# A rotary embedding kernel: one queue for all loads with a new opening, and five tiles added on TensorE instead of four

## The chip, the cores and the metric

The kernel runs on one core of a Trainium2 chip. Times are device microseconds (us) of one execution. A run is called fast or slow by its time against the fastest of the same kernel; only fast runs are compared. The kernel before takes 164.6 us; one of its first three runs took 231.49 us and is not used.

A core has five engines with instruction streams of their own: TensorE (PE in the profile), VectorE (DVE), ScalarE (ACT), GpSimd (POOL) and SyncE (SP). Here SyncE and ScalarE also issue the transfers between HBM and on-chip memory; 16 DMA engines carry them out.

## The reference

```
x: (8, 2048, 8, 64) float32      cos, sin: (2048, 32) float32
x1, x2 = x[..., :32], x[..., 32:]
out1 = x1 * cos - x2 * sin
out2 = x1 * sin + x2 * cos
return concatenate([out1, out2], axis=-1)
```

The tables depend on the position alone and are shared by batch and heads. 33.55 MB are read as x, 0.52 MB as tables, and 33.55 MB written.

## The kernel before

x is cut into 16 slabs of 2 MB (128 partitions x 4096 elements), each rotated in place in one of nine buffers and stored from there. A slab is two tiles of 2048 columns. A tile of kind "A" is done by GpSimd (x times sin, the two halves exchanged, into `t2`) and DVE (x times cos into `t1`, then `t1 + t2`). For kind "B" TensorE adds instead, by two products with the identity summed in PSUM, and ScalarE copies the sum back in four copies. For kind "C" DVE makes both products and TensorE adds them, so GpSimd does nothing.

```
    NBUF = 9                         # slab buffers
    ...
    def cuts(i):                     # how slab i is loaded; HD = 512 columns, UNIT = 2048
        if i == 0:
            return [HD, HD, 2 * HD, UNIT]
        return [SLAB]

    def pieces(i):                   # how slab i is computed (and the last one stored)
        if i == 0:
            return [HD, HD, 2 * HD, UNIT]
        if i == last:
            return [UNIT, 2 * HD, HD, HD]
        return [UNIT, UNIT]
    ...
    nc.scalar.dma_start(out=cos_sb, in_=cos_src)
    for i in range(NBUF):
        load(i)                      # on nc.sync; sin comes right after the first piece of slab 0
    ...
    kinds = {}
    for i in (5, 10):
        kinds |= {(i, 0): "C", (i, UNIT): "B"}
    ...
            # in rotate(), kind "B"; "C" is alike
            for j in range(n // C):
                ...
                nc.tensor.matmul(o, eye, t1[:, cs], start=True, stop=False)
                nc.tensor.matmul(o, eye, t2[:, cs], start=False, stop=True)
                keep(nc.scalar.copy(xt[:, cs], o))
    ...
    LAG = 2

    def store(i, lo, n):             # on ScalarE's DMA queue
        keep(nc.scalar.dma_start(out=ov[...], in_=xts[i][:, lo : lo + n]))

    for i in range(last + 1):
        if i == last:
            for k in range(i - LAG, i):
                store(k, 0, SLAB)
        for lo, n in spans(pieces(i)):
            rotate(i, lo, n)
            if i == last:
                store(i, lo, n)
        if LAG <= i < last:
            store(i - LAG, 0, SLAB)
        if i > LAG and i - LAG - 1 + NBUF <= last:
            load(i - LAG - 1 + NBUF)
```

ScalarE takes its instructions in order, so the store of slab 3, which the program writes after `rotate(5)`, stands behind the eight copies of slab 5. And load 9 needs the buffer of slab 0, so it waits until store 0 has landed, and so on.

Of the kernel before, what the change touches and what calls it, by code (L numbers as in the profile page):

```python
# [10 lines left out]
def kernel(  # L11
# [7 lines left out]
    nc = tc.nc  # L19
# [4 lines left out]
    B, S, H, D = x.shape  # L24
    Dh = D // 2
    P = 128
    HD = H * D
# [4 lines left out]
    SLAB = SL * HD  # L32
    UNIT = 4 * HD
# [5 lines left out]
    cos_src = cos.rearrange("(q r) d -> q r d", q=P)  # L39
# [10 lines left out]
    cos_sb = const_pool.tile([P, R, Dh], f32, tag="cb")  # L50
# [9 lines left out]
    xts = {}  # L60

    def cuts(i):
        if i == 0:
            return [HD, HD, 2 * HD, UNIT]
        return [SLAB]

    def pieces(i):
        if i == 0:
            return [HD, HD, 2 * HD, UNIT]
        if i == last:  # L70
            return [UNIT, 2 * HD, HD, HD]
        return [UNIT, UNIT]

    def spans(sizes):
        lo = 0
        for n in sizes:
            yield lo, n
            lo += n

    def load(i):  # L80
        b, l = slabs[i]
        xt = xpool.tile([P, SLAB], f32, tag="xt", name=f"xt{i}")
        for lo, n in spans(cuts(i)):
            nc.sync.dma_start(
                out=xt[:, lo : lo + n],
                in_=xv[b, :, l * SLAB + lo : l * SLAB + lo + n],
            )
            if i == 0 and lo == 0:
                nc.sync.dma_start(out=sin_sb, in_=sin_src)
        xts[i] = xt  # L90

    nc.scalar.dma_start(out=cos_sb, in_=cos_src)
    for i in range(NBUF):
        load(i)

# [2 lines left out]
        out=eye,  # L98
        in_=eye,
# [12 lines left out]
        return dataclasses.replace(a, ap=[a.ap[0][:], a.ap[1][:], [0, n], a.ap[-1][:]])  # L112

    kinds = {}
    for i in (5, 10):
        kinds |= {(i, 0): "C", (i, UNIT): "B"}

    def rotate(i, lo, n):
        b, l = slabs[i]
# [69 lines left out]
# [12 lines that stand above are left out]
# [30 lines left out]
```

## Time and profile before

| | before |
|---|---|
| time, median | 164.63 us |
| span of the profiled execution | 163.0 us |
| moved by DMA | 67.66 MB |
| DVE busy / GpSimd busy / ScalarE busy / TensorE busy | 143.4 / 139.4 / 12.0 / 33.3 us |

First the busy tenths of DVE and of the 16 DMA engines, and the rate, in 40 equal slices of the span (4.08 us each):

```profile
DVE  0587999999999999999899999999999999999900
...
DMA  4999999999999999999999999999999999999995
GB/s 137 383 432 442 406 398 426 438 438 418 438 434 426 430 434 430 426 434 438 422 428 438 424 422 446 430 414 446 434 422 430 442 422 422 446 426 430 434 402 207
```

The DMA engines are at 90% or more in every slice but the first and the last. The same as windows; columns are the stretch, its length, the busy time of the engines, the granted TensorE clock, the DMA share and the rate:

```profile
core 0: us, PE busy (x) PEld busy (x) DVE busy (x) ACT busy (x) POOL busy (x), PEclk, DMA share, GB/s
20.00:24.00 4.00, 0.00 (x0) 0.00 (x0) 3.86 (x3) 0.00 (x0) 4.00 (x3) 1.00 0.97 377
66.00:72.00 6.00, 6.00 (x15) 2.66 (x14) 5.83 (x4) 2.35 (x4) 5.05 (x3) 1.00 1.01 434
126.00:132.00 6.00, 0.00 (x0) 0.00 (x0) 5.88 (x3) 0.00 (x0) 6.00 (x3) 0.50 1.01 431
136.00:156.00 20.00, 0.00 (x0) 0.00 (x0) 18.10 (x12) 0.00 (x0) 12.93 (x10) 0.50 1.00 430
```

The stretch from 136 to 156 us has only stores, that from 66 to 72 only loads: 430 to 434 GB/s either way. That is the limit. The Trainium skill, page "DMA: Bandwidth & Descriptors", Specifications, gives 435 GB/s as the fabric's ceiling, and this trace agrees. (Slices and short windows can read more, because a packet counts whole where it starts.) 67.66 MB at 430 GB/s are 157.3 us. Below, "lost" time is worked out from the trace's DMA packets so: the length of a stretch, less the bytes moved in it divided by 429.5 GB/s, an estimate of the sustained rate, close to the 430 from 136 to 156 us. Before loses 3.2 us while starting, 0.44 us in a slow patch from 19.75 to 21.75, 0.7 us at the end, and nothing else.

Next ScalarE's timeline: start, length, and what it was. A line with ACTq is a group of DMA issues, its length the time from the first issue to the end of the last.

```profile
17.85 19.24 ACTq L183 DMA_DIRECT2D out_dram<-xt  x3
62.24 0.59 ACT L176 COPY xt<-o 128x512 f32<-128x512 f32 x1 [55.27 <-DVE t L144]
...
74.83 0.59 ACT L158 COPY xt<-o 128x512 f32<-128x512 f32 x1 [1.13 <-PE o L157]
74.83 6.93 ACTq L183 DMA_DIRECT2D out_dram<-xt  x5
106.85 0.59 ACT L176 COPY xt<-o 128x512 f32<-128x512 f32 x1 [31.44 <-PE o L173]
...
119.32 0.59 ACT L158 COPY xt<-o 128x512 f32<-128x512 f32 x1 [1.13 <-PE o L157]
119.38 35.97 ACTq L183 DMA_DIRECT2D out_dram<-xt  x11
```

Three stores are issued by 37 us. The next leave at 74.83, with the last copy of slab 5: 38 us without a store. The same happens before 119.38. Nothing is lost, because loads are still queued: the trace's landings have load 11, the last that could be queued without store 3, land at 79.74, and the last load of all at 123.86. The margins are 4.9 and 4.5 us. The loads do wait for stores; here is the largest entry of SyncE's own waits (total us, times, longest):

```profile
SPq L84 <- DMA out_dram<-xt: 86.4, 7, 31.9
```

### The profile page before, as it was taken

How to read it: one execution, taken by the hardware profiler on the slowest of the kernel's cores; microseconds unless marked ns; L12 is line 12 of the kernel's file. 1: busy time of each engine (PE TensorE's matmuls, PEld its weight loads, DVE VectorE, ACT ScalarE, POOL GpSimd, SP SyncE). 2: the span in 40 equal slices, each digit the busy share in tenths (PEclk: the TensorE clock that was granted, in tenths of full speed). 3: DMA queues.
4: the chain of work that ended last, by engine and by line, in shares of the span. 5: the costliest groups of instructions: out<-in, count | busy, mean ns of one | idle time of the engine just before them, and what ended most of it. 6: DMA issues, size and time to landing. Idle time of an engine off the chain costs nothing. (4 is left out here: it accounts for less than half of the span.)

```text
span 163.0 us, 480 instructions
## 1 busy us (share of the span) xinstructions
PE 33.3 (20%) x64; PEld 13.4 (8%) x64; DVE 143.4 (88%) x71; ACT 12.0 (7%) x20; POOL 139.4 (86%) x74
## 2 busy tenths in 40 slices
PE   0000000000000079993000000899920000000000
PEld 0000000000000024440000000244400000000000
DVE  0587999999999999999899999999999999999900
ACT  3300000000000002232000000022410000000000
POOL 1599999999999999799999999956999999995000
PEclk9999999999999999999555555579997555555555
DMA  4999999999999999999999999999999999999995
GB/s 137 383 432 442 406 398 426 438 438 418 438 434 426 430 434 430 426 434 438 422 428 438 424 422 446 430 414 446 434 422 430 442 422 422 446 426 430 434 402 207
DMA packets 5763, 67.66 MB, mean 415 GB/s; under 512 B 640, under 2 KB 640, under 8 KB 1664
## 3 DMA queue, kind: packets, MB, share of 16 engines
q1 hardware_dynamic: 2880, 33.82, 49.5%
q10 hardware_dynamic: 2880, 33.82, 48.7%
q14 instruction: 3, 0.02, 0.0%
HBM read 34.08 MB, written 33.55 MB: 415 GB/s over the span
## 5 line engine op out<-in xcount | busy, mean ns | idle before, releaser
L138 POOL TENSOR_TENSOR t<-xt,sin_sb 128x1024 f32<-128x1024 f32 (+2 forms) x34 | 70.7, 2081 | 10.8 <-DVE xt L151 6.3
L144 DVE TENSOR_TENSOR t<-xt,cos_ps 128x2048 f32<-128x2048 f32 (+2 forms) x36 | 73.9, 2056 | 1.0
L138 POOL TENSOR_TENSOR t<-xt,nsin 128x1024 f32<-128x1024 f32 (+2 forms) x34 | 70.8, 2082 | 0.0
L151 DVE TENSOR_TENSOR xt<-t,t 128x2048 f32<-128x2048 f32 (+2 forms) x32 | 64.8, 2025 | 5.6 <-POOL t L138 2.1
L172 PE MATMUL o<-t,eye 128*128 128x512 f32 x16 | 11.3, 800 | 85.8 <-DVE t L144 85.8
L176 ACT COPY xt<-o 128x512 f32<-128x512 f32 x8 | 4.7, 586 | 94.5 <-DVE t L144 55.3
L172 PEld LDWEIGHTS o<-t,eye 128*128 128x128 f32 x16 | 3.9, 256 | 90.6 <-issue 90.6
L156 PE MATMUL o<-t,eye 128*128 128x512 f32 x16 | 8.2, 592 | 0.0
L157 PE MATMUL o<-t,eye 128*128 128x512 f32 x16 | 8.2, 592 | 0.0
L173 PE MATMUL o<-t,neye 128*128 128x512 f32 x8 | 6.2, 862 | 0.2 <-DVE t L161 0.2
L158 ACT COPY xt<-o 128x512 f32<-128x512 f32 x8 | 4.7, 586 | 9.0 <-PE o L157 9.0
L108 DVE COPY cos_ps<-cos_sb 128x512 f32<-128x512 f32 x1 | 0.7, 694 | 5.0 <-DMA cos_sb<-in_cos_dram 5.0
L161 DVE TENSOR_TENSOR t<-xt,sin_ps 128x2048 f32<-128x2048 f32 x2 | 4.6, 2281 | 0.0
L173 PE MATMUL o<-t,eye 128*128 128x512 f32 x8 | 4.1, 592 | 0.0
L157 PEld LDWEIGHTS o<-t,eye 128*128 128x128 f32 x16 | 3.0, 190 | 3.8 <-issue 3.8
L156 PEld LDWEIGHTS o<-t,eye 128*128 128x128 f32 x16 | 3.0, 190 | 3.8 <-issue 3.8
L173 PEld LDWEIGHTS o<-t,neye 128*128 128x128 f32 x8 | 2.0, 278 | 4.9 <-issue 3.3
L173 PEld LDWEIGHTS o<-t,eye 128*128 128x128 f32 x8 | 1.5, 190 | 1.9 <-issue 1.9
L106 ACT ACT_TABLE_LOAD x1 | 1.3, 1283 | 1.2 <-PEq L215 1.2
L106 ACT ACTIVATE nsin<-sin_sb 128x512 f32<-128x512 f32 x1 | 0.6, 630 | 3.2 <-DMA sin_sb<-in_sin_dram 3.2
L109 ACT COPY sin_ps<-sin_sb 128x512 f32<-128x512 f32 x1 | 0.6, 579 | 0.0
L96 POOL MEMSET eye<- 128x128 f32 x1 | 0.2, 205 | 0.3 <-POOLq L215 0.3
(6 smaller groups left out, 1.0 us busy)
## 6 DMA issues: line engine op xcount, KB each, us to landing
xt<-in_x_dram SPq DMA_DIRECT2D x15, 2048.0 KB, 27.6
out_dram<-xt ACTq DMA_DIRECT2D x15, 2048.0 KB, 15.3
xt<-in_x_dram SPq DMA_DIRECT2D x1, 1024.0 KB, 7.8
out_dram<-xt ACTq DMA_DIRECT2D x1, 1024.0 KB, 10.3
xt<-in_x_dram SPq DMA_DIRECT2D x2, 256.0 KB, 4.3
xt<-in_x_dram SPq DMA_DIRECT2D x1, 512.0 KB, 5.8
out_dram<-xt ACTq DMA_DIRECT2D x1, 512.0 KB, 8.9
out_dram<-xt ACTq DMA_DIRECT2D x2, 256.0 KB, 7.6
```

Source lines behind the costliest of these rows:

```text
L106: nc.scalar.mul(nsin, sin_sb, -1.0)
L108: nc.vector.tensor_copy(cos_ps, cos_sb)
L138: nc.gpsimd.tensor_mul(out=t2u[:, :, u, :].rearrange("p (r h) d -> p r h d", h=H), in0=xu[:, :, 1 - u, :].rearrange("p (r h) d -> p r h d" ...
L144: nc.vector.tensor_mul(out=t1.rearrange("p (r k d) -> p r k d", r=nr, d=Dh), in0=xk, in1=rep(cos_ps[:, r0 : r0 + nr, :], 2 * H),)
L151: keep(nc.vector.tensor_add(out=xt, in0=t1, in1=t2))
L156: nc.tensor.matmul(o, eye, t1[:, cs], start=True, stop=False)
L157: nc.tensor.matmul(o, eye, t2[:, cs], start=False, stop=True)
L158: keep(nc.scalar.copy(xt[:, cs], o))
L161: nc.vector.tensor_mul(out=t2.rearrange("p (r k d) -> p r k d", r=nr, d=Dh), in0=xk, in1=rep(sin_ps[:, r0 : r0 + nr, :], 2 * H),)
L172: nc.tensor.matmul(o, eye, t1u[:, gs, u, :], start=True, stop=False)
L173: nc.tensor.matmul(o, eye if u else neye, t2u[:, gs, 1 - u, :], start=False, stop=True)
L176: keep(nc.scalar.copy(xu[:, gs, u, :], o.rearrange("p (g d) -> p g d", d=Dh)))
```

## The change

The intent, as far as the diff tells it: larger first loads in one queue, no DMA issue on ScalarE at the start, and a fifth tile taken off DVE.

```diff
     def cuts(i):
-        if i == 0:
-            return [HD, HD, 2 * HD, UNIT]
-        return [SLAB]
+        return [UNIT, UNIT] if i == 0 else [SLAB]
     def pieces(i):
         if i == 0:
-            return [HD, HD, 2 * HD, UNIT]
+            return [2 * HD, 2 * HD, UNIT]
         if i == last:
-            return [UNIT, 2 * HD, HD, HD]
+            return [UNIT, 2 * HD, 2 * HD]
 ...
             if i == 0 and lo == 0:
+                nc.sync.dma_start(out=cos_sb, in_=cos_src)
                 nc.sync.dma_start(out=sin_sb, in_=sin_src)
 ...
-    nc.scalar.dma_start(out=cos_sb, in_=cos_src)
 ...
-    for i in (5, 10):
+    for i in (4, 11):
         kinds |= {(i, 0): "C", (i, UNIT): "B"}
+    kinds[(8, 0)] = "B"
```

## The prediction

> **What bounds the kernel now.** The 16 DMA engines. The page's slices show DMA at 90% or more in all but the first and last of 40, and windows from 8 us on move 420 to 450 GB/s whether loads, stores or both run. 67.66 MB at about 429 GB/s is 157.5 us of the 163.0 us span. The Trainium skill ("DMA: Bandwidth & Descriptors", Specifications) gives 435 GB/s as fabric ceiling; the trace agrees. Compute is nearly as long (DVE 143.4 us, GpSimd 139.4 us) but ends at 155.0, with some 6 us of stores still queued. So DVE time saved is worth nothing by itself; the queues must never run dry.
>
> **Why they could.** A load from slab 9 on needs an earlier store to land, and ScalarE issues stores in order, behind its PSUM copies. Timeline: stores of slabs 0 to 2 issue at 17.9, 27.3, 36.8, then none until 74.8, behind the eight copies of slab 5 (62.2 to 75.4, 1.72 us apart, paced by TensorE). The queued loads last until 79.7. It repeats with slab 10: stores 8 and later wait until 119.4; the last load lands at 123.9. Margins of 4 to 5 us.
>
> **What the change does.**
> 1. Start: x comes as 1 MB, with cos and sin behind it. The skill (same page, "Issuing engines are not separate DMA queues") says other issuing engines save only issue time: here 0.41 us. But sin, which GpSimd needs, has 1.57 MB ahead of and in it, not 0.79: I expect its landing near 7.2 us (5.6 before), and the first slab done about 1.5 us later. Larger packets fill the ramp 0.3 us better.
> 2. One more tile added on TensorE: 2.3 us off DVE, four copies (about 8 us with TensorE's slow start) on ScalarE.
> 3. The blocked stretches move. ScalarE's built order: stores 0, 1, copies of slab 4, stores 2 to 5, copies of slab 8, stores 6 to 8, copies of slab 11, stores 9 on.
>
> **Costing it.** I carried the measured pitches (4.73 us per 2048-column tile on DVE, 4.57 on GpSimd, 1.72 per copy) and 429 GB/s through both orders; for before this gives store 8 at 118.6 (measured 119.4).
> - First dry point: only loads 0 to 10 and stores 0, 1 can be queued, 13 slabs, gone near 68. Store 2 issues near 67. Margin about zero: 0 to 1 us idle.
> - Slab 8: stores 6 to 8 issue near 93. No loss.
> - Second: all 16 loads and stores 0 to 8, gone near 127. Slab 11 is one slab later than slab 10 was; the copies end near 127.5, so store 9 starts moving near 129. About 2 us idle. This decides: from there seven stores, 14.7 MB, 34.2 us, and about 1 us to land.
> Last landing near 164.2 instead of 162.2.
>
> **Prediction:** 166.5 us (+1.1%); 8 in 10 between 164.4 and 168.2. Faster by over 2%: 0.01; within 2%: 0.86; slower by over 2%: 0.13.
>
> **What would show it.** Right: the slices show DMA dipping near 127 to 129 us and perhaps near 68; no store issues between about 94 and 127; DVE ends near 153; sin lands about 1.5 us later. Wrong: DMA at 9 throughout and about 164.3 us.
>
> **What would make it wrong.** The margins are estimates of about 1 us. If the first slab is done as early as before, or the copies run faster, the gaps close and the time stays at 164.3. If copies of slab 11 start later (GpSimd setting the pace and eating the DVE saving), the gap grows by as much, to 168 or more.

## The result, and the profile after

The changed kernel takes 167.5 us (167.31 to 167.66, four runs). The ratio to before is 1.0175 (95% interval 1.0155 to 1.0195). Ratios here are the mean time of one kernel's fast runs over the mean of the other's fast runs of the same rounds, so they are not quite the ratio of the medians quoted. The prediction was 166.5 us with a range of 164.4 to 168.2, and within 2%: it held, and the time was 1 us above its centre.

The same lines of the page, after (slices of 4.15 us):

```profile
DVE  0449999999999999999999999999999999999000
...
DMA  5999999999999999999999999999998999999995
GB/s 186 417 457 423 419 312 443 435 439 431 407 439 443 435 435 411 387 439 399 403 443 419 419 415 435 435 431 431 415 435 344 379 439 395 431 443 439 397 408 212
```

DMA dips to 8 in slice 31, where the rate is 344 GB/s and then 379; slice 6 has 312. ScalarE's timeline:

```profile
19.29 9.79 ACTq L182 DMA_DIRECT2D out_dram<-xt  x2
54.16 0.58 ACT L175 COPY xt<-o 128x512 f32<-128x512 f32 x1 [45.97 <-PE o L172]
...
67.15 0.58 ACT L157 COPY xt<-o 128x512 f32<-128x512 f32 x1 [1.13 <-PE o L156]
67.16 4.91 ACTq L182 DMA_DIRECT2D out_dram<-xt  x4
88.55 0.59 ACT L157 COPY xt<-o 128x512 f32<-128x512 f32 x1 [20.81 <-DMA out_dram<-xt]
...
94.55 0.58 ACT L157 COPY xt<-o 128x512 f32<-128x512 f32 x1 [1.13 <-PE o L156]
94.56 3.29 ACTq L182 DMA_DIRECT2D out_dram<-xt  x3
115.08 0.58 ACT L175 COPY xt<-o 128x512 f32<-128x512 f32 x1 [19.94 <-PE o L172]
118.03 0.58 ACT L175 COPY xt<-o 128x512 f32<-128x512 f32 x1 [2.37 <-PE o L172]
...
128.33 0.58 ACT L157 COPY xt<-o 128x512 f32<-128x512 f32 x1 [1.13 <-PE o L156]
128.39 25.29 ACTq L182 DMA_DIRECT2D out_dram<-xt  x9
```

The stretches without a store are now from 29.08 to 67.16 and from 97.85 to 128.39 (the ends of the issues before them are from the trace). The same four windows as before:

```profile
20.00:24.00 4.00, 0.00 (x0) 0.00 (x0) 3.88 (x2) 0.00 (x0) 4.00 (x3) 1.00 1.03 324
66.00:72.00 6.00, 1.12 (x3) 0.19 (x1) 5.86 (x3) 0.61 (x2) 6.00 (x3) 0.80 1.00 390
126.00:132.00 6.00, 2.29 (x6) 0.75 (x4) 5.66 (x4) 1.17 (x2) 6.00 (x4) 0.92 0.79 330
136.00:156.00 20.00, 0.00 (x0) 0.00 (x0) 16.68 (x10) 0.00 (x0) 11.71 (x8) 0.50 1.02 432
```

Between 126 and 132 us the rate is 330 instead of 431. In windows of 1 us it reads 279 from 127, 0 from 128, and 508 from 129. By the packets, no data packet starts from 127.97 to 129.23, and none is in flight from 128.6 to 129.2.

The balance, as lost time in us (worked out from the packets as above):

| stretch | before | after | difference |
|---|---|---|---|
| opening, to 8 us | 3.23 | 2.46 | -0.77 |
| slow patch after the first store (20 to 25) | 0.44 | 1.11 | +0.67 |
| at store 2 (68.25 to 69.75) | 0 | 0.49 | +0.49 |
| at 78.25 to 79.5 | 0 | 0.27 | +0.27 |
| hole at store 9 (127.5 to 129.5) | 0 | 1.36 | +1.36 |
| last packets, and all small losses | 0.7 | 1.2 | +0.5 |
| last packet ends at | 161.85 | 164.40 | +2.55 |

The last but one row is what the others leave. The difference of the medians is 2.9 us. The rows say where time was lost, not what each cure would give back: bytes that did not move before 127 us are still queued then, so an early loss should make the hole behind slab 11 shorter (argued, not tested alone).

The opening did move the start of compute, as GpSimd's first product shows, before and then after:

```profile
5.74 0.72 POOL L138 TENSOR_TENSOR t<-xt,sin_sb 128x256 f32<-128x256 f32 x1 [4.44 <-DMA sin_sb<-in_sin_dram]
```

```profile
7.00 2.47 POOL L137 TENSOR_TENSOR t<-xt,sin_sb 128x512 f32<-128x512 f32 x2 [5.70 <-DMA sin_sb<-in_sin_dram]
```

It waits for sin in both, 1.26 us longer after. The first slab is done, and its store issued, at 19.29 instead of 17.85.

### The profile page after: what moved, and what is told of

Read it like the earlier page. It is cut to its first block, busy times and chain, and to the rows that moved or that the text cites. A ratio compares the mean times of both kernels' runs of the same rounds, so it can differ in the third digit from the quotient of the medians.

```text
span 165.8 us, 498 instructions
## 1 busy us (share of the span) xinstructions
PE 44.2 (27%) x80; PEld 17.8 (11%) x80; DVE 140.3 (85%) x66; ACT 14.3 (9%) x24; POOL 138.9 (84%) x70
## 5 line engine op out<-in xcount | busy, mean ns | idle before, releaser
L137 POOL TENSOR_TENSOR t<-xt,sin_sb 128x1024 f32<-128x1024 f32 (+1 forms) x32 | 70.5, 2205 | 8.2 <-DMA sin_sb<-in_sin_dram 5.7
L143 DVE TENSOR_TENSOR t<-xt,cos_ps 128x2048 f32<-128x2048 f32 (+1 forms) x34 | 73.4, 2167 | 0.9
L137 POOL TENSOR_TENSOR t<-xt,nsin 128x1024 f32<-128x1024 f32 (+1 forms) x32 | 70.7, 2209 | 0.0
L150 DVE TENSOR_TENSOR xt<-t,t 128x2048 f32<-128x2048 f32 (+1 forms) x29 | 62.2, 2144 | 5.9 <-POOL t L137 2.5
L171 PE MATMUL o<-t,eye 128*128 128x512 f32 x16 | 12.0, 843 | 66.3 <-DVE t L143 66.3
L155 PE MATMUL o<-t,eye 128*128 128x512 f32 x24 | 14.2, 676 | 17.6 <-DVE t L143 17.6
L156 PE MATMUL o<-t,eye 128*128 128x512 f32 x24 | 13.2, 633 | 0.0
L171 PEld LDWEIGHTS o<-t,eye 128*128 128x128 f32 x16 | 3.9, 257 | 71.3 <-issue 71.3
L175 ACT COPY xt<-o 128x512 f32<-128x512 f32 x8 | 4.7, 585 | 74.9 <-PE o L172 74.9
L157 ACT COPY xt<-o 128x512 f32<-128x512 f32 x12 | 7.0, 585 | 34.1 <-DMA out_dram<-xt 20.8
L155 PEld LDWEIGHTS o<-t,eye 128*128 128x128 f32 x24 | 5.0, 212 | 24.3 <-issue 24.3
L172 PE MATMUL o<-t,neye 128*128 128x512 f32 x8 | 6.8, 943 | 0.1
L156 PEld LDWEIGHTS o<-t,eye 128*128 128x128 f32 x24 | 5.0, 210 | 6.9 <-issue 6.9
L172 PE MATMUL o<-t,eye 128*128 128x512 f32 x8 | 4.1, 592 | 0.0
L172 PEld LDWEIGHTS o<-t,eye 128*128 128x128 f32 x8 | 1.5, 190 | 1.9 <-issue 1.9
```

What stands on the lines that cost most here:

```text
L137: nc.gpsimd.tensor_mul(out=t2u[:, :, u, :].rearrange("p (r h) d -> p r h d", h=H), in0=xu[:, :, 1 - u, :].rearrange("p (r h) d -> p r h d" ...
L143: nc.vector.tensor_mul(out=t1.rearrange("p (r k d) -> p r k d", r=nr, d=Dh), in0=xk, in1=rep(cos_ps[:, r0 : r0 + nr, :], 2 * H),)
L150: keep(nc.vector.tensor_add(out=xt, in0=t1, in1=t2))
L171: nc.tensor.matmul(o, eye, t1u[:, gs, u, :], start=True, stop=False)
L172: nc.tensor.matmul(o, eye if u else neye, t2u[:, gs, 1 - u, :], start=False, stop=True)
L175: keep(nc.scalar.copy(xu[:, gs, u, :], o.rearrange("p (g d) -> p g d", d=Dh)))
```

## The experiments

The theory: DMA is the limit; the changed order makes ScalarE issue stores so late that the queues run dry, above all behind the copies of slab 11. Rival A: the later opening (1.4 us) makes everything later. Rival B: the fifth tile itself costs the time, by its TensorE and ScalarE work or by a lower clock.

All twelve runs gave results equal to the reference's.

### Stores ahead of the copies (e1)

The same work on every engine. Only ScalarE's order changes: a slab that has a TensorE tile (4, 8, 11) is preceded by every store that is ready.

```diff
+    nxt = 0
     for i in range(last + 1):
-        if i == last:
-            for k in range(i - LAG, i):
-                store(k, 0, SLAB)
+        if i == last or kinds.get((i, 0)):
+            while nxt < i:
+                store(nxt, 0, SLAB)
+                nxt += 1
 ...
-        if LAG <= i < last:
-            store(i - LAG, 0, SLAB)
+        if LAG <= i < last and nxt <= i - LAG:
+            store(nxt, 0, SLAB)
+            nxt += 1
```

> The changed kernel, but each slab with a TensorE tile (4, 8, 11) is preceded in ScalarE's order by every store that is ready, instead of followed by it; TensorE, DVE and GpSimd do the same work. Theory (queues run dry behind the copies): no hole in DMA near 68 and near 128, store 9 issues near 106 instead of 128, time 163.6 to 164.3 us, below the kernel before because the opening ramp stays 0.8 us better. Rival A (the later opening makes all later): still 167. Rival B (the added TensorE tile, its copies or the lower clock cost the time): still 167.

Measured: 164.61 us (164.47 to 164.74), ratio to before 0.9998 (0.9983 to 1.0013). The page's DMA lines and the stores on ScalarE's timeline:

```profile
DMA  5999999999999999999999999999999999999994
GB/s 183 419 445 435 435 318 423 439 427 443 423 435 431 423 439 431 419 443 427 427 439 427 437 425 427 435 427 439 427 423 439 431 427 435 427 443 423 429 408 200
```

```profile
19.31 28.69 ACTq L182 DMA_DIRECT2D out_dram<-xt  x4
...
67.05 15.76 ACTq L182 DMA_DIRECT2D out_dram<-xt  x4
...
94.44 14.48 ACTq L182 DMA_DIRECT2D out_dram<-xt  x3
115.11 0.59 ACT L175 COPY xt<-o 128x512 f32<-128x512 f32 x1 [20.70 <-PE o L172]
...
127.61 0.59 ACT L157 COPY xt<-o 128x512 f32<-128x512 f32 x1 [1.13 <-PE o L156]
128.23 25.48 ACTq L182 DMA_DIRECT2D out_dram<-xt  x7
```

The copies of slab 11 run at the same time as in the changed kernel (115.11 to 128.20, against 115.08 to 128.91), but stores 8 to 10 were issued between 94.44 and 108.92, so DMA has work: no slice but the ends is below 9. TensorE is busy 42.0 us (44.2 in the changed kernel), ScalarE 14.3 in both, and the first slab is as late (store 0 at 19.31). So neither the fifth tile nor the late opening costs the time; both rivals fall as the main cause.

Nor does the clock cost it by itself. In the changed kernel TensorE began slab 11 slowly: the granted clock was 0.50 from 115 to 117 us, and the first two copies are 2.95 us apart, where 1.72 is the steady spacing. e5 (below: e1 with cos on ScalarE's queue) begins slab 11 as slowly, with the same clock and copies 2.97 us apart, and still moves 431 GB/s between 126 and 132 us. But with the stores behind the copies the slow start counts: by these spacings it put off store 9 by 1.2 us (an estimate), and 1.36 us were lost in that execution.

The time lies above the range expected (163.6 to 164.3), because the gain over before did not come: the opening is 0.8 us better, but the slow patch at 21.5 to 24.5 takes 0.97 us where before lost 0.44. In the profiled run the last packet ends 0.5 us earlier than before's (161.35); of that the medians keep 0.1.

### Only slab 11's stores ahead (e9)

```diff
-        if i == last or kinds.get((i, 0)):
+        if i in (11, last):
```

(against e1; slabs 4 and 8 keep the changed order)

> The changed kernel with only stores 9 and 10 moved ahead of the copies of slab 11; slabs 4 and 8 keep the changed order. Theory: the hole at 127.5 to 129.5 (1.4 us) goes, the slow patches near 68 and 78 (0.75 us) stay: 165.5 to 166.3 us. If the hole near 128 was only a symptom of what happened at 68: no gain, 167.

Measured: 165.59 us (165.46 to 166.16), ratio 1.0064 (1.0038 to 1.0091). Two windows:

```profile
66.00:72.00 6.00, 0.66 (x2) 0.00 (x0) 5.86 (x3) 0.59 (x1) 6.00 (x3) 0.73 0.99 423
126.00:132.00 6.00, 1.84 (x5) 0.53 (x3) 5.66 (x4) 1.17 (x2) 5.83 (x4) 0.85 0.99 423
```

Stores 9 and 10 left at 99.49 and 108.52, the hole at 128 is gone (423 against 330 GB/s), and the median is 1.9 us lower. So the hole is not a mere symptom of what happened near 68, where the edit changes nothing. Not all of the 1.9 us need be the hole's, though. In this execution store 2 left at 66.71, not at 67.16, and the loss near 68 stayed away too (423 against 390 GB/s), which was not expected. The last packet ends 1.87 us earlier than in the changed kernel's trace; the hole had cost 1.36 us there and the loss near 68 0.49. The margin near 68 is that thin. What differs is how slowly TensorE begins after idling: the first two copies of slab 4 are 2.69 us apart in the changed kernel's trace, 2.27 in that of e9, 1.95 in that of e1, and 1.72 is the steady spacing.

### Without the tile in slab 8 (e4)

```diff
-    kinds[(8, 0)] = "B"
```

> The changed kernel without the fifth tile (first half of slab 8), so less TensorE and ScalarE work and 2.3 us more on DVE. Theory: slab 11 is reached about 2.7 us later, store 9 issues near 131, the hole grows to about 4 us: 169.5 to 170.5 us. Rival B (the added tile costs the time): faster than 167.5, toward 165. Rival A: 167.5.

Measured: 168.6 us (167.85 to 169.48), ratio 1.0242 (1.0196 to 1.0288). By the page and the timeline:

```profile
DMA  5999999999999999999999999999993699999996
GB/s 184 422 453 426 422 324 430 426 426 434 434 430 434 434 434 426 430 430 391 422 422 432 436 418 434 434 430 418 418 438 145 281 406 438 438 438 434 406 410 250
```

```profile
130.75 25.25 ACTq L181 DMA_DIRECT2D out_dram<-xt  x9
```

Less work on TensorE and ScalarE (and more on DVE) made it slower still, as the theory said and rival B denied: DVE's 2.3 us return before slab 11, stores 9 to 12 leave from 130.75, and 4.26 us are lost between 127.0 and 131.75 (1.36 in the changed kernel). The size was overstated: the median lies 0.9 us below the range expected. The trace shown is of the slowest of four runs. So the fifth tile, taken by itself, helps: it brings slab 11 forward. What hurts is where the pairs stand: e2, next, has the same opening and four tiles in slabs 5 and 10 and takes 165 us.

### The old tiles with the new opening (e2), the new tiles with the old opening (e3)

e2 is the changed kernel with `for i in (5, 10)` and no tile in slab 8; e3 is the kernel before with `for i in (4, 11)` and the tile in slab 8.

> The changed opening and pieces, with the old four TensorE tiles (slabs 5 and 10). Theory: store 8 issues near 120.5 with the loads lasting to about 121, so a hole of 0 to 1.5 us in all: 164.0 to 165.4 us. Rival A (the opening costs it): 167 or more. Rival B (the tiles cost it): 163.8.

> The old opening and pieces, with the five TensorE tiles of the change. Theory: compute is 1.4 us earlier, so store 9 issues near 126.5 and the hole there shrinks from 1.4 to about 0.5 us: 165.0 to 166.0 us. Rival A (the opening costs it): 164.6. Rival B (tiles): 167.

e2: the profiled execution (169.64 us) is not read. The four fast runs are 164.75 to 165.68, ratio 1.0027 (0.9998 to 1.0057). So the opening does not explain the 2.9 us: rival A falls here too. e3: 165.71 us (164.88 to 166.13), ratio 1.0058 (1.0026 to 1.009), inside the range expected. But its profiled execution is its fastest (164.88) and shows no hole. In it TensorE began slab 11 without a slow start (the granted clock was 1.00 from 115 to 117 us): the first two copies are 1.72 us apart, and store 9 left at 125.78. In the changed kernel's trace they are 2.95 apart.

```profile
113.70 0.59 ACT L178 COPY xt<-o 128x512 f32<-128x512 f32 x1 [19.27 <-PE o L175]
115.42 0.58 ACT L178 COPY xt<-o 128x512 f32<-128x512 f32 x1 [1.13 <-PE o L175]
...
125.78 3.20 ACTq L185 DMA_DIRECT2D out_dram<-xt  x4
```

Store 9 left 2.6 us earlier than in the changed kernel, 1.4 by the opening and 1.2 by the quick start. That the slower runs of e3 have the hole is argued, not shown.

### The order of stores where there was no hole (e11)

The edit of e1, made to the kernel before.

> The kernel before with its stores moved ahead of the copies in the same way as e1. It had no hole in DMA, so the theory gives nothing to win: 164.5 to 164.8 us, no hole, loss of 0.4 us near 20 as before. If issuing stores early is worth something by itself: below 164.2.

Measured: 164.86 us (164.62 to 164.97), ratio 1.0011 (0.9996 to 1.0027). Early stores were worth nothing by themselves here; they paid where the queues would run dry. Its slow patch cost 0.67, more than the 0.4 expected.

### The slow patch after the first store (e5 to e8, e10, e12)

The balance showed a loss that nobody had predicted: some 2 us after the first store is issued, the loads in flight slow down for 2 to 3 us, before the first store's packets show (in the changed kernel the store is issued at 19.29 and its first packet starts at 23.80; until then single packets of 16 KB take up to 1.36 us instead of 0.61). Six runs tried to move it. All but e6 start from e1.

e8 exchanges stores 0 and 1, so the first store leaves at 29.0 us:

```diff
+        if i == LAG + 1:
+            store(1, 0, SLAB)
+            store(0, 0, SLAB)
+            nxt = 2
-        if LAG <= i < last and nxt <= i - LAG:
+        elif LAG + 1 < i < last and nxt <= i - LAG:
```

> e1 with stores 0 and 1 exchanged, so that the first store is issued at 28.8 us instead of 19.3. If the slow patch belongs to the first store, it moves to about 31 to 34 us; if it belongs to the loads in flight at that time, it stays at 21.5 to 24.5. No verdict on time is asked.

e5 undoes one part of the change, e6 does so without e1's order, and e7 issues a tiny store early:

```diff
 e5 and e6
-                nc.sync.dma_start(out=cos_sb, in_=cos_src)
+    nc.scalar.dma_start(out=cos_sb, in_=cos_src)      # before the loads
 e7
+    warm = const_pool.tile([P, 4], f32, tag="warm")
+    nc.vector.memset(warm, 0.0)
+    nc.scalar.dma_start(out=ov[0, :, 0:4], in_=warm)  # overwritten by store 0
```

> e1 with one part of the change undone: cos is again loaded by ScalarE's queue. Question: in every kernel with the new opening the loads run slowly for 3 us (about 1.0 us of transfer lost, 21.5 to 24.5) about 2 us after the first store is issued; with the old opening it is 2 us (about 0.5 lost). Theory Q (the first use of ScalarE's DMA queue costs it, and cos used to be that use): the loss falls to about 0.5 and the time to 164.0. Rival (it comes with the order and size of the first loads): still 1.0 lost, 164.6.

> The changed kernel with cos back on ScalarE's queue and nothing else. Whatever it does to the early slow patch, the hole near 128 is set by when store 9 is issued, so what is won early is lost there: 167.2 to 167.6, the hole larger by the gain. If the early loss counted in the changed kernel by itself: 166.9 or less.

> e1 with a 2 KB store (128 partitions of 16 bytes, overwritten later by slab 0) issued on ScalarE's queue within the first us, before there is load traffic. Theory Q: the slow patch at 21.5 falls from 1.0 us lost to 0.5 or less (below 0.2 if the first write matters too): 163.7 to 164.2. Rival: 1.0 lost still, 164.6.

e10 stores slab 0 in its three pieces as they are ready; e12 issues the same three pieces in reverse order, the 1 MB one first, when slab 0 is done:

```diff
 e10
-            if i == last:
+            if i in (0, last):
                 store(i, lo, n)
 e12
+        if i == 0:
+            for lo, n in reversed(list(spans(pieces(0)))):
+                store(0, lo, n)
```

> e1 with slab 0 stored in three pieces (512 KB, 512 KB, 1 MB), the first issued near 12 us. The slow patch belongs to the first store: it should start near 14 us. If it is a cost of the first time the queue is filled, whatever the size, it is again about 1.0 us and the time 164.6; if it grows with the first store's size, it is 0.5 or less and the time 164.0 to 164.3.

> e10 with the three stores of slab 0 in reverse order, so that the first of them (1 MB) is issued at 19.3 us as in e1, not at 12. If smaller first stores cure the slow patch (its length goes with the first store's size): loss near 0.5 us or less, time 164.1 to 164.3. If the earlier time cured it: loss 0.9 to 1.0 us again, time 164.6.

Windows of e1, then e8, then e10, then e12:

```profile
20.00:24.00 4.00, 0.00 (x0) 0.00 (x0) 3.90 (x2) 0.00 (x0) 4.00 (x3) 1.00 1.02 332
```

```profile
20.00:24.00 4.00, 0.00 (x0) 0.00 (x0) 3.90 (x2) 0.00 (x0) 4.00 (x3) 1.00 1.05 446
32.00:34.00 2.00, 0.00 (x0) 0.00 (x0) 1.97 (x2) 0.00 (x0) 2.00 (x2) 1.00 0.88 270
```

```profile
20.00:24.00 4.00, 0.00 (x0) 0.00 (x0) 3.90 (x2) 0.00 (x0) 4.00 (x3) 1.00 1.04 441
```

```profile
20.00:24.00 4.00, 0.00 (x0) 0.00 (x0) 3.90 (x2) 0.00 (x0) 4.00 (x3) 1.00 0.98 350
```

In e8 the slow stretch has left 20 to 24 us (446 GB/s) and stands at 32 to 34 (270). In e10 this stretch is undisturbed (441); its packets lose 0.23 us before it, thinly spread, where e1 loses nothing. In e12 the slow stretch is smaller (350 against 332 in e1).

| run | first store: issued, size | slow patch | lost, us | time, us | ratio to before |
|---|---|---|---|---|---|
| before | 17.85, 2 MB | 19.75 to 21.75 | 0.44 | 164.6 | 1 |
| e1 | 19.31, 2 MB | 21.5 to 24.5 | 0.97 | 164.61 | 0.9998 |
| e5, cos on ScalarE | 19.81, 2 MB | 22.0 to 24.25 | 0.68 | 164.42 | 0.9986 |
| e6, cos on ScalarE | 19.53, 2 MB | 22.0 to 24.5 | 0.77 | 167.04 | 1.0140 |
| e7, early 2 KB store | 19.52, 2 MB | 22.0 to 24.5 | 1.00 | 164.58 | 0.9995 |
| e8, stores exchanged | 29.00, 2 MB | 31.25 to 34.0 | 0.99 | 164.48, one run | |
| e10, pieces | 12.01, 512 KB | spread, 14.5 to 19 | 0.23 | 164.07 | 0.9967 |
| e12, pieces late | 19.43, 1 MB | 21.5 to 23.75 | 0.60 | 164.00 | 0.9957 |

What follows, with the losses from one execution each: the patch belongs to the first store, not to the loads of that moment (e8). It is smaller if that store is smaller (e12, at the same time), and smallest if the first store is 512 KB and early (e10). The tiny store does not remove it (e7). With cos on ScalarE's queue it cost 0.68 and 0.77 us (e5, e6), against 0.97 or more in every other trace with the new opening and a first store of 2 MB; that is less of a cure than theory Q expected. The edit also changes the order of the first loads, so the queue is not shown to be the reason, and no gain in time is shown: the interval of e5 (0.9973 to 0.9998) overlaps that of e1. Why a first large store slows loads is not settled by these runs. In e6 the median fell by 0.46 us, below the range expected. Its profiled execution is the slowest of five (167.81) and has the hole near 128 (1.52 us lost); with fast runs from 166.89 to 167.81 this one is inconclusive.

e10 and e12 beat both kernels: the intervals of their ratios are 0.9952 to 0.9982 and 0.9940 to 0.9973. The gain is about 0.4%.

## Why the prediction was right

- **"The 16 DMA engines" bound the kernel, and DVE time saved is worth nothing.** Right. e1 ends at the old time with DVE 3 us less busy, 140.3 against 143.4.
- **The second dry point decides; store 9 near 127.5, about 2 us idle.** Right in place and mechanism; 1.36 us were lost. Moving only the stores in front of slab 11 gave back 1.9 us (e9, with the reservation made there). Store 9's first packet started at 129.23, and 35.6 us remained to the last landing (164.79); the estimate was 34.2 and about 1 from near 129. That the 129 fits so well is partly luck: the copies ended at 128.91, not near 127.5, but store 9 left at 128.39, while the last copy ran, and moved 0.3 us after the end of the copies, where 1.5 had been allowed.
- **The first dry point, 0 to 1 us.** Right in size: 0.49 us in the profiled run, none in e9. In kind it was not idle time but slow packets at the first of the stores (up to 1.53 us instead of 0.61, with all 16 DMA engines busy).
- **Slab 8 costs nothing.** Right, and e4 shows that without it the time rises.
- **sin near 7.2 us, first slab 1.5 us later.** sin landed at 6.86; the first store left 1.44 us later.
- **"Larger packets fill the ramp 0.3 us better."** Mis-sized: the ramp is 0.77 us better. That larger packets are the reason was not tested alone.
- **Missing from the sum:** the slow patches, 0.67 us more at the first store and 0.27 at 78. Its "420 to 450 GB/s" from 8 us on passes over the 377 between 20 and 24 us. On the prediction's own path these losses lie before store 9 and shorten the hole instead of adding to the time, which fits a hole of 1.36 us where 2 were forecast; no run tests that alone. The microsecond between 166.5 and 167.5 lies behind: 0.2 us because store 9 moved at 129.23, 0.4 from there to the last landing, and the rest after it (the profiled execution, 167.6 us, took 2.8 us there; the forecast allows 2.3).
- **"Other issuing engines save only issue time."** The prediction took this from the skill, and no run here contradicts it: with cos back on ScalarE's queue the median was 0.2 us lower (e5 against e1), with overlapping intervals.

## What to carry to other kernels

Where DMA is the limit and compute nearly as long, ask of every change how long the queued transfers last against the longest stretch in which none can be issued. Here two stretches had 4.9 and 4.5 us of slack; moving tiles by one slab used that up, with less DVE work and no wait that named the cause. Where a queue shares an in-order engine with compute, try issuing what is ready before the compute, not after it; here that cured the loss at no cost. A loss seen only as a slower rate, without a wait, is found by adding up the bytes.

## What the Trainium skill lacked or had wrong

- "DMA: Bandwidth & Descriptors" has nothing on loads slowing after a queue's first large store: 0.44 to 1.11 us lost some 2 us after the issue of a first store of 2 MB, 0.60 with 1 MB, 0.23 with 512 KB issued at 12 us.
- The same page, "Issuing engines are not separate DMA queues": the passage, that the choice of engine saves only issue time, says nothing of an issuing engine that also computes. Here no store left ScalarE for 30 us (97.85 to 128.39), while its PSUM copies stood in front, and 1.9 us came back when stores 9 and 10 went first (e9).
- The same page, "Where 436 GB/s comes from", says that for transfers between HBM and SBUF the HBM side (about 358) binds, although it also reports 425 for a 16 MB load. Here such transfers ran at 430 to 434 GB/s, loads or stores alone. "HBM Reference", Specifications (TRN2), has it better: about 425 for a core streaming alone.
- The same page, "Rules for kernel authors", asks for 1 MiB or more per DMA for the most bandwidth. It does not mention that the first store may be an exception: storing slab 0 as 512 KB, 512 KB and 1 MB took 164.07 us (164.00 with the 1 MB first), against 164.61 as 2 MB.
